# A decoder step on one core: dense activations kept in PSUM, low halves moved to GpSimd, and a gather tile with one buffer fewer

## The chip, the cores and the metric

One Trainium2 chip, one of its cores. The metric is the device time of one execution in microseconds (us), the median of several runs. In the text PE is the matrix engine, DVE the vector engine, ACT the scalar engine, POOL the GpSimd engine and SP the queue that issues most loads.

## What is computed

A decoder layer for 1024 prompt tokens and 8 samples of 8 tokens (1088 tokens, 9 tiles: 0 to 7 are prompt, 8 is the 64 sample tokens): RMSNorm, two recurrent mixers (retention and RWKV-7) with one output projection, then the PEER expert mixer, then a gated per-layer input, then a final norm. The change lies in the PEER part:

```
def block(xb):
    q = (xb @ wq).reshape(PEER_BLOCK, PEER_HEADS, 2, PEER_DKEY // 2)
    s = jnp.einsum('phcd,hcnd->phcn', q, keys)
    sv, si = lax.top_k(s, PEER_TOPK)
    ...                        # the best 16 of 16 x 16 pairs give e, an expert number out of 16384
    gsm = jax.nn.softmax(cv, axis=-1)
    hval = jnp.einsum('pd,phkd->phk', xb, u_tab[e])
    act = gelu(hval) * gsm
    return jnp.einsum('phk,phkd->pd', act, v_tab[e])
```

Each token picks 8 x 16 experts; each expert is a row of 1024 numbers in `u_tab` (peer_u) and one in `v_tab` (peer_v).

## The kernel before

All data are fp32; a product that must be exact to fp32 is made of three fast products of a high and a low half (`mm3`, L325 to L327). A half pair comes from `split` (L296 ACT copies to the rounded type, then L298 on DVE or L300 on POOL subtracts to get the low half).

The PEER part is done in two ways:

- **Gathered.** For tiles 0, 1, 8 (list `E0`, run by `early` beside the mixers) and 2, 3 (`G1`, run later), `gather` fetches for each of a token's 128 experts one row per token by an indirect DMA that POOL issues (L1127, 128 rows of 4 KB into a buffer `grow`), and DVE multiplies and sums it (L1141 for peer_u, L1155 for peer_v; the running sum `gacc` lies in PSUM). Tile 8 needs 64 rows a table, the others 128. In all 576 rows of each table. The buffers that `grow` rotates through are shared with the query and top-k work of the early tiles: tile 0 uses the tags V (two buffers), W and xy, tiles 1 and 8 those and xT, which is also the buffer of the transposed input in the query of tile 8 and of `eq` in its top-k.
- **Dense.** For tiles 4 to 7 (`G2`, 512 tokens) all 128 x 128 experts are multiplied and weighted by a mostly zero gate matrix. `hidden` makes gelu(u x) for 128 experts at once (24 matmuls into `ph`, L1265 gelu to `geh`). The first 96 of the 128 blocks (`NPRE`) are made early and stored to DRAM (`gd`). `gates` builds the gate matrix of a tile in 32 steps of 4 tokens: two one-hot tiles on DVE (L1241), four scalings on ACT (L1243), four matmuls `pwt` (L1246), one copy (L1247), and stores it to DRAM (`wd`). Its SBUF pool `gw` opens where the early gather's pool is closed, and its first copy (`it`, L1234) follows. Then `dense_fused` makes the last 32 blocks and uses them at once; `dense_stored` loads the 96 others again (`ge`). `act` multiplies by the gate (L1275) and splits into `ah` and `al` (L296, L298); `dense` loads a piece of peer_v (`vraw`), splits it into `vh` and `vl`, and multiplies (`py`, L1300: 12 matmuls each in the fused part, 15 in the stored one, 224 `py` in all), and DVE adds `py` to `yT` (L1307).

`ple` is the last part. The program is written as generators; a scheduler of the language puts the instructions of each engine in an order by priority (the order of the text) and by its own costs, and that order is then fixed. On the chip each engine runs its list in order and waits on semaphores. An SBUF buffer of a closed pool is handed on tile by tile, with a wait.

Of the kernel before, what the change touches and what calls it, by code (L numbers as in the profile page):

```python
# [8 lines left out]
F32 = mybir.dt.float32  # L9
# [162 lines left out]
GHB = 2  # L172
# [38 lines left out]
class K:  # L211
# [117 lines left out]
    def group(self, tiles):  # L329
        self.tiles = tiles  # L330
        self.off, self.ntok = spans(tiles)
        self.chunks = chunks_of(self.ntok)
# [878 lines left out]
    def early(self, wp):  # L1211

        rows = ("V", "V", "W", "xy")
        yield from self.early_query(wp, E0[0], "V", 2, ("W", "Wq"))
        g = self.gather(wp, E0[0], rows, acc=self.acc)
        for t in E0[1:]:
            while t not in self.rowed:
                next(g, None)
                yield
            for _ in self.early_query(wp, t, "Wq", 1, ("Wq", "xT")):  # L1220
                next(g, None)
                yield
        yield from g
        for t in E0[1:]:
            yield from self.gather(wp, t, rows + ("xT",), acc=self.acc)
# [26 lines left out]
    def hidden(self, dp, ep, x, i1):  # L1252

        nc, I = self.nc, self.I
        ch = self.chunks
        raw = dp.tile([128, 8, 128], F32, name="uraw", bufs=UB)
        nc.sync.dma_start(raw, I['puT'][i1])
        uh = dp.tile([128, 8, 128], F32R, name="uh", bufs=DW)
        ul = dp.tile([128, 8, 128], F32R, name="ul", bufs=DW)
        self.split(uh, ul, raw, "g")  # L1260
        ge = ep.tile([128, self.ntok], F32, name="geh", bufs=GHB)
        for c0, cn in ch:
            p = self.psh.tile([128, 512], F32, name="ph")
            self.mm3(p[:, :cn], lambda k: uh[:, k, :], lambda k: ul[:, k, :], lambda k: x[0][:, k, c0:c0 + cn], lambda k: x[1][:, k, c0:c0 + cn], 8)
            nc.scalar.activation(ge[:, c0:c0 + cn], p[:, :cn], AF.Gelu)  # L1265
        return ge

    def act(self, dl, dr, i1, ge):
        nc = self.nc
# [11 lines left out]
    def dense(self, dl, dr, yT, groups, acts_of, side):  # L1281
        nc, I = self.nc, self.I
        ch = self.chunks
        cw = ch[0][1]
        ncx = len(ch)
        for g0, nb in groups:
            acts = acts_of(g0, nb)
            for d in range(8):
# [5 lines left out]
                self.split(vh, vl, raw, "g" if d % 2 else "v")  # L1294
                p = self.ps2.tile([128, ncx, 512], F32, name="py")
                for b in range(nb):
                    ah, al = acts[b]
                    for j, (lh, rh) in enumerate(((vh, ah), (vh, al), (vl, ah))):
                        for c, (c0, cn) in enumerate(ch):
                            nc.tensor.matmul(p[:, c, :cn], lh[:, b, :], rh[:, c0:c0 + cn], start=b == 0 and j == 0,  # L1300
                                             stop=b == nb - 1 and j == 2)
                pv = p[:, :ncx, :cw]
                yv = yT[:, d, :].rearrange("p (c n) -> p c n", c=ncx)
                if self.first:
                    nc.vector.tensor_copy(yv, pv)
                else:
                    nc.vector.tensor_tensor(yv, yv, pv, op=OP.add)  # L1307
            self.first = False

    def dense_fused(self, dl, dr, hp, x, yT):  # L1310
# [112 lines left out]
    def build(self):  # L1423
# [3 lines left out]
        with self.es:  # L1427
# [94 lines left out]
            with ExitStack() as e:  # L1522
                dl = sb("dl", e, bufs=2)
                yT = sb("dy", e, side="right").tile([128, 8, self.ntok], F32, name="yT")
                with ExitStack() as e2:
                    self.ps2 = self.pool("psumy", bufs=4 // len(self.chunks), space=PS, es=e2, reuse_waits="tile")
                    dr = sb("dr", e2, bufs=2, side="right")
                    with ExitStack() as e3:
                        self.psh = self.pool("psumh2", bufs=2, space=PS, es=e3, reuse_waits="tile")
                        self.dense_fused(dl, dr, da, x, yT)  # L1530
# [20 lines left out]
```

## Time and profile before

| | |
|---|---|
| median of 3 runs | 4120.41 us (4110.44 to 4128.16) |
| the profiled execution | 4119.08 us, of which the span from first to last instruction is 4117.0 us |
| mean granted PE clock | 0.858 |
| busy over the span | PE 84%, DVE 77%, POOL 54%, ACT 28% |
| DMA | 1107 MB, 269 GB/s over the span |

An engine's busy time counts its own instructions, not its waits. PE's matmuls overlap one another, so that a group's mean duration (0.4 us) is longer than the distance from one to the next (0.23 us); a sum over PE is therefore made from counts per microsecond. The parts of the span, by the first matmul of each kind: the mixers, the early tiles and the query of the others to 1997 us; hidden products, top-k and gates to 2953 us; the fused dense part to 3265 us; the stored part to 3949 us; the last part to 4117 us.

### The profile page before, as it was taken

What the parts mean: (1) busy time and instruction counts of PE and PEld (TensorE: products, weight loads), DVE (VectorE), ACT (ScalarE), POOL (GpSimd) and SP (SyncE); (2) the same over time, 40 slices, a digit from 0 to 9 for tenths busy, and PEclk for the clock granted to TensorE, in tenths of its full rate; (3) what the DMA queues carried; (4) which work ended last, traced back from release to release, by engine and by line L of the source; (5) the groups of instructions that cost most, each with busy time, mean ns of one, the idle gap of its engine ahead of it and who ended that gap; (6) DMA issues with size and microseconds to landing.
All of it is one profiled execution on the core that took longest, in us unless ns stands there. A gap on an engine that the chain in (4) does not pass through costs nothing. (4 is left out here: it accounts for less than half of the span.)

```text
span 4117.0 us, 52401 instructions
## 1 busy us (share of the span) xinstructions
PE 3449.2 (84%) x17749; PEld 2831.4 (69%) x17749; DVE 3165.3 (77%) x5876; ACT 1172.9 (28%) x2149; POOL 2212.5 (54%) x1939
## 2 busy tenths in 40 slices
PE   8789977777779888849998989856699988888988
PEld 7688976546658766638877767745588766666767
DVE  4453579877881588776799988898799989999844
ACT  4232211111111111112222325767422222222222
POOL 5353265544451155545678888643477666666410
PEclk9799986577775678769999999866799999999999
DMA  7267478899772368899988888888899999999822
GB/s 254 77 205 231 143 254 271 280 285 289 262 245 81 102 215 303 301 347 342 335 266 311 300 292 301 322 323 301 302 325 339 333 339 352 351 350 361 311 90 68
DMA packets 473862, 1107.18 MB, mean 269 GB/s; under 512 B 74555, under 2 KB 191545, under 8 KB 467642
## 3 DMA queue, kind: packets, MB, share of 16 engines
q0 software_dynamic: 165888, 604.05, 41.3%
q1 hardware_dynamic: 245694, 393.26, 29.3%
q10 hardware_dynamic: 62012, 106.52, 7.0%
q8 instruction: 140, 2.29, 0.2%
q14 instruction: 128, 1.05, 0.1%
HBM read 997.17 MB, written 106.43 MB: 268 GB/s over the span
## 5 line engine op out<-in xcount | busy, mean ns | idle before, releaser
L1127 POOL DMA_INDIRECT grow<-in_pv,eid x576 | 588.2, 1021 | 529.8 <-DVE gacc L1155 359.7
L1127 POOL DMA_INDIRECT grow<-in_pu,eid x576 | 580.2, 1007 | 480.7 <-DVE grow L1141 342.3
L1155 DVE SCALAR_TENSOR_TENSOR gacc<-grow,ac,gacc 128x1024 f32<-128x1024 f32 x571 | 732.4, 1283 | 109.7 <-DMA grow<-in_pv,eid 103.5
L1141 DVE SCALAR_TENSOR_TENSOR grow<-grow,gacc 128x1024 f32<-128x1024 f32 x576 | 689.5, 1212 | 57.8 <-DMA grow<-in_pu,eid 53.4
L1300 PE MATMUL py<-ah,vl 128*128 128x512 f32 x1024 | 412.1, 408 | 49.4 <-DVE vl L298 32.0
L1300 PE MATMUL py<-ah,vh 128*128 128x512 f32 x1024 | 413.0, 407 | 38.4 <-ACT ah L296 25.2
L325 PE MATMUL ph<-cx,uh 128*128 128x512 f32 x1024 | 409.8, 400 | 23.2 <-ACT geh L1265 14.7
L327 PE MATMUL ph<-cx,ul 128*128 128x512 f32 x1024 | 406.6, 399 | 19.5 <-POOL ul L300 19.5
L1300 PE MATMUL py<-al,vh 128*128 128x512 f32 x1024 | 411.5, 402 | 3.1 <-DVE al L298 3.1
L326 PE MATMUL ph<-cx,uh 128*128 128x512 f32 x1024 | 406.4, 397 | 0.0
L300 POOL TENSOR_TENSOR ul<-uraw,uh 128x1024 fp32r<-128x1024 f32 x128 | 307.2, 2401 | 29.5 <-ACT uh L296 27.5
L1246 PE MATMUL pwt<-oh,oh 128*128 128x128 f32 x1024 | 202.5, 365 | 122.8 <-ACT oh L1243 105.1
L1246 PEld LDWEIGHTS pwt<-oh,oh 128*128 128x128 f32 x1024 | 182.9, 260 | 143.9 <-ACT oh L1243 141.8
L1300 PEld LDWEIGHTS py<-ah,vl 128*128 128x128 f32 x1024 | 196.6, 192 | 118.8 <-DVE vl L298 51.8
L1300 PEld LDWEIGHTS py<-ah,vh 128*128 128x128 f32 x1024 | 197.4, 193 | 100.7 <-ACT vh L296 32.7
L325 PEld LDWEIGHTS ph<-cx,uh 128*128 128x128 f32 x1024 | 196.7, 192 | 68.7 <-ACT geh L1265 17.4
L327 PEld LDWEIGHTS ph<-cx,ul 128*128 128x128 f32 x1024 | 196.6, 192 | 67.7 <-POOL ul L300 26.4
L300 POOL TENSOR_TENSOR vl<-vraw,vh 128x640 fp32r<-128x640 f32 (+2 forms) x112 | 171.1, 1527 | 128.8 <-ACT vh L296 126.1
L296 ACT ACTIVATE uh<-uraw 128x1024 fp32r<-128x1024 f32 x128 | 135.5, 1059 | 360.3 <-DMA uraw<-in_puT 276.9
L1300 PEld LDWEIGHTS py<-al,vh 128*128 128x128 f32 x1024 | 197.1, 193 | 50.7 <-DVE al L298 8.0
L296 ACT ACTIVATE vh<-vraw 128x640 fp32r<-128x640 f32 (+2 forms) x224 | 149.6, 686 | 272.8 <-PE py L1300 202.5
L326 PEld LDWEIGHTS ph<-cx,uh 128*128 128x128 f32 x1024 | 197.1, 192 | 41.2
(402 smaller groups left out, 7959.7 us busy)
## 6 DMA issues: line engine op xcount, KB each, us to landing
uraw<-in_puT SPq DMA_DIRECT2D x128, 512.0 KB, 5.0
vraw<-in_pvd SPq DMA_DIRECT2D x152, 320.0 KB, 5.3
cw<-in_w_out SPq DMA_DIRECT2D x128, 256.0 KB, 5.3
wd<-wst ACTq DMA_DIRECT2D x32, 1024.0 KB, 11.2
wt<-wd SPq DMA_DIRECT2D x64, 512.0 KB, 6.7
wraw<-in_w_ret SPq DMA_DIRECT2D x48, 512.0 KB, 4.8
ewq<-in_wq SPq DMA_DIRECT2D x48, 512.0 KB, 4.4
gd<-geh ACTq DMA_DIRECT2D x96, 256.0 KB, 5.1
```

The source lines that it names most:

```text
L296: nc.scalar.activation(hi, src, AF.Copy)
L300: nc.gpsimd.tensor_tensor(lo, src, hi.bitcast(F32), op=OP.subtract)
L325: mm(out, lh(k), rh(k), start=first and k == 0, stop=False)
L326: mm(out, lh(k), rl(k), start=False, stop=False)
L327: mm(out, ll(k), rh(k), start=False, stop=last and k == nk - 1)
L1127: nc.gpsimd.indirect_dma_start(out=g, out_offset=None, in_=src, in_offset=bass.IndirectOffsetOnAxis(ap=self.eid[t][:, j:j + 1], axis=0))
L1141: nc.vector.scalar_tensor_tensor(g[:, c], g[:, c], 1.0, x[:, c], op0=OP.mult, op1=OP.mult, accum_out=hv[:, i, j:j + 1])
L1155: nc.vector.scalar_tensor_tensor(y[:, c], g[:, c], ac[:, j:j + 1], y[:, c], op0=OP.mult, op1=OP.add)
L1246: nc.tensor.matmul(pw[:, j, :], oh[1][:, j, :], oh[0][:, j, :], start=True, stop=True)
L1300: nc.tensor.matmul(p[:, c, :cn], lh[:, b, :], rh[:, c0:c0 + cn], start=b == 0 and j == 0, stop=b == nb - 1 and j == 2)
```

## The change

Three things are done at once.

1. **Tile 1's gather** no longer takes a fifth buffer with the tag xT; tile 8's still does. Tile 1 now rotates through four.
2. **Activations from PSUM.** In the fused part the gelu writes back into its PSUM tile `ph`, and the gate product and the split read it there. In the stored part the loaded `ge` is first copied by ACT into such a PSUM tile (a new instruction for each of 96 blocks). There are three `ph` and three `py` PSUM tiles in the whole dense part; before there were two `ph` in the fused part alone and four `py`. In the hidden stage (96 blocks) the gelu still goes to SBUF.
3. **peer_v's low halves** `vl` are all made by POOL. Before, DVE and POOL took every other one (112 each).

```diff
@@ early
         for t in E0[1:]:
-            yield from self.gather(wp, t, rows + ("xT",), acc=self.acc)
+            yield from self.gather(wp, t, rows + ("xT",) * (t == E0[-1]), acc=self.acc)
@@ hidden
-        ge = ep.tile([128, self.ntok], F32, name="geh", bufs=GHB)
-        for c0, cn in ch:
-            p = self.psh.tile([128, 512], F32, name="ph")
...
-            nc.scalar.activation(ge[:, c0:c0 + cn], p[:, :cn], AF.Gelu)
+        p = self.psh.tile([128, self.ntok], F32, name="ph")
+        self.mm3(p, lambda k: uh[:, k, :], lambda k: ul[:, k, :], lambda k: x[0][:, k], lambda k: x[1][:, k], 8)
+        ge = ep.tile([128, self.ntok], F32, name="geh", bufs=GHB) if ep else p
+        nc.scalar.activation(ge, p, AF.Gelu)
@@ dense
-                self.split(vh, vl, raw, "g" if d % 2 else "v")
+                self.split(vh, vl, raw, "g")
@@ dense_fused
-                made[b] = self.act(dl, dr, b, self.hidden(hp, dr, x, b))
+                made[b] = self.act(dl, dr, b, self.hidden(hp, None, x, b))
@@ dense_stored
                 self.nc.sync.dma_start(ge, self.gd[b])
-                out.append(self.act(dl, dr, b, ge))
+                p = self.psh.tile([128, self.ntok], F32, name="ph")
+                self.nc.scalar.activation(p, ge, AF.Copy)
+                out.append(self.act(dl, dr, b, p))
@@ build
-                    self.ps2 = self.pool("psumy", bufs=4 // len(self.chunks), space=PS, es=e2, reuse_waits="tile")
+                    self.ps2 = self.pool("psumy", bufs=3, space=PS, es=e2, reuse_waits="tile")
+                    self.psh = self.pool("psumh2", bufs=3, space=PS, es=e2, reuse_waits="tile")
```

What this does to the order of the instructions is shown at three places.

**POOL, in the mixers, behind the last rows of tile 0** (`eid_65` is the list of tile 1's experts; hnr, kk, k, rk, Z, hnx and the like belong to the mixers). Before, four rows of tile 1 are issued, then none until the query and top-k of tile 8 are through:

```order
L1127 DMA grow<-in_pu,eid_65 128x1024 x4
L290 TENSOR_SCALAR crs<-cssq 128x1
L736 COPY pe<-Pa 128x4
L735 COPY pe<-Pi 128x4
L291 TENSOR_TENSOR crs<-crs,halves 128x1
L745 TENSOR_TENSOR kk<-ft,vec 128x512
L752 TENSOR_TENSOR k_9766<-ft,m_9761 128x512
L756 TENSOR_TENSOR rk_9770<-ft,vec 128x512
L757 TENSOR_TENSOR rk_9770<-rk_9770,k_9766 128x512
L783 TENSOR_TENSOR k_9766<-k_9766,Pi 128x512
```

With the change, a little further down the same stretch:

```order
L1126 DMA grow<-in_pu,eid_65 128x1024 x18
L290 TENSOR_SCALAR hnr<-hnss 128x8
L291 TENSOR_TENSOR hnr<-hnr,halves 128x8
L1126 DMA grow<-in_pu,eid_65 128x1024 x3
L970 TENSOR_TENSOR hnx<-hnx,row_ln_g 128x512
L1126 DMA grow<-in_pu,eid_65 128x1024
L971 TENSOR_TENSOR hnx<-hnx,row_ln_b 128x512
L1126 DMA grow<-in_pu,eid_65 128x1024
L974 TENSOR_TENSOR hnx<-hnx,bv 128x512
L825 TENSOR_TENSOR Z<-Z,csta 128x1024
L1126 DMA grow<-in_pu,eid_65 128x1024 x67
```

Rows of tile 1 fill the stretch in which there were none. Where the first hidden block's low half stands on POOL, 577 rows have been issued, 472 before. Where the first `vl` stands, it is 777 rows, 799 before.

**PE, in the hidden stage, at the second tile's gates** (`ph` are hidden products, `pit` the transposed gate input of a tile, `pwt` the gate products). Before, 2018 of the `ph` matmuls stand ahead of the first `pwt`, and here all of the 96 hidden blocks are already done, so that the `pwt` follow each other:

```order
L326 MATMUL ph<-cx_13026,uh 128x512
L327 MATMUL ph<-cx_13025,ul 128x512
L1246 MATMUL pwt<-oh_17197,oh_17198 128x128
L1232 MATMUL pit<-csta,e_17212 128x128 x2
L1232 MATMUL pit<-csta,gsm 128x128
L1246 MATMUL pwt<-oh_17197,oh_17198 128x128 x3
L1246 MATMUL pwt<-oh_18860,oh_18861 128x128 x4
```

With the change 847 `ph` stand ahead of the first `pwt`, and the gates lie between hidden products:

```order
L325 MATMUL ph<-cx_13025,uh 128x512
L326 MATMUL ph<-cx_13026,uh 128x512
L1245 MATMUL pwt<-oh_17197,oh_17198 128x128 x4
L1231 MATMUL pit<-csta,e_17212 128x128 x2
L1231 MATMUL pit<-csta,gsm 128x128
L327 MATMUL ph<-cx_13025,ul 128x512
L325 MATMUL ph<-cx_13025,uh 128x512
L326 MATMUL ph<-cx_13026,uh 128x512
```

From the first `pwt` to the last there are now some 1529 `ph`; the last 60 of the 512 `pwt` stand alone. On DVE the first gate instruction stands, in both programs, just behind the last row of tile 8.

**POOL, in the stored dense part** (`vl` low halves, `grow` rows of tile 3, `eid_68`, `pgb` weights of the last part). Before, one `vl` for two to three rows:

```order
L300 TENSOR_TENSOR vl<-vraw,vh 128x640
L1127 DMA grow<-in_pv,eid_68 128x1024 x2
L300 TENSOR_TENSOR pgb<-pgr,pgb 128x512
L1127 DMA grow<-in_pv,eid_68 128x1024 x3
L300 TENSOR_TENSOR vl<-vraw,vh 128x640
```

With the change:

```order
L300 TENSOR_TENSOR vl<-vraw,vh 128x640
L1126 DMA grow<-in_pv,eid_68 128x1024
L300 TENSOR_TENSOR vl<-vraw,vh 128x640 x2
L1126 DMA grow<-in_pv,eid_68 128x1024 x2
L300 TENSOR_TENSOR vl<-vraw,vh 128x640
```

Two `vl` for each one, and the rows reach to the end: sixteen rows of tile 3 stand behind the last `vl`; before, the last row stood at the 98th of POOL's 112 `vl`.

More of the change, by code (lines that the diff above doesn't have):

```diff
@@ L331, in group @@
         self.off, self.ntok = spans(tiles)
-        self.chunks = chunks_of(self.ntok)
     def a_pool(self, es, name):
@@ L1254, in hidden @@
         nc, I = self.nc, self.I
-        ch = self.chunks
         raw = dp.tile([128, 8, 128], F32, name="uraw", bufs=UB)
@@ L1260, in hidden @@
         self.split(uh, ul, raw, "g")
-        ge = ep.tile([128, self.ntok], F32, name="geh", bufs=GHB)
-        for c0, cn in ch:
-            p = self.psh.tile([128, 512], F32, name="ph")
-            self.mm3(p[:, :cn], lambda k: uh[:, k, :], lambda k: ul[:, k, :], lambda k: x[0][:, k, c0:c0 + cn], lambda k: x[1][:, k, c0:c0 + cn], 8)
-            nc.scalar.activation(ge[:, c0:c0 + cn], p[:, :cn], AF.Gelu)
+        p = self.psh.tile([128, self.ntok], F32, name="ph")
+        self.mm3(p, lambda k: uh[:, k, :], lambda k: ul[:, k, :], lambda k: x[0][:, k], lambda k: x[1][:, k], 8)
+        ge = ep.tile([128, self.ntok], F32, name="geh", bufs=GHB) if ep else p
+        nc.scalar.activation(ge, p, AF.Gelu)
         return ge
@@ L1282, in dense @@
         nc, I = self.nc, self.I
-        ch = self.chunks
-        cw = ch[0][1]
-        ncx = len(ch)
         for g0, nb in groups:
@@ L1293, in dense @@
                 vl = dl.tile([128, NB, 128], F32R, name="vl")[:, :nb]
-                self.split(vh, vl, raw, "g" if d % 2 else "v")
-                p = self.ps2.tile([128, ncx, 512], F32, name="py")
+                self.split(vh, vl, raw, "g")
+                p = self.ps2.tile([128, self.ntok], F32, name="py")
                 for b in range(nb):
@@ L1298, in dense @@
                     for j, (lh, rh) in enumerate(((vh, ah), (vh, al), (vl, ah))):
[L1299 to L1303, printed above, removed]
+                        nc.tensor.matmul(p, lh[:, b, :], rh, start=b == 0 and j == 0, stop=b == nb - 1 and j == 2)
                 if self.first:
-                    nc.vector.tensor_copy(yv, pv)
+                    nc.vector.tensor_copy(yT[:, d, :], p)
                 else:
-                    nc.vector.tensor_tensor(yv, yv, pv, op=OP.add)
+                    nc.vector.tensor_tensor(yT[:, d, :], yT[:, d, :], p, op=OP.add)
             self.first = False
@@ L1525, in build @@
                 with ExitStack() as e2:
-                    self.ps2 = self.pool("psumy", bufs=4 // len(self.chunks), space=PS, es=e2, reuse_waits="tile")
+                    self.ps2 = self.pool("psumy", bufs=3, space=PS, es=e2, reuse_waits="tile")
+                    self.psh = self.pool("psumh2", bufs=3, space=PS, es=e2, reuse_waits="tile")
                     dr = sb("dr", e2, bufs=2, side="right")
-                    with ExitStack() as e3:
-                        self.psh = self.pool("psumh2", bufs=2, space=PS, es=e3, reuse_waits="tile")
-                        self.dense_fused(dl, dr, da, x, yT)
+                    self.dense_fused(dl, dr, da, x, yT)
                     self.dense_stored(dl, dr, yT, self.ple_weights(cx, da, dl))
```

## The prediction

> **What bounds the kernel now.** I read the span by stages first (engine busy time, granted clock, DMA share), then how many gather rows POOL issues in each, then the waits and the groups of the two stages that the change touches.
>
> ```profile
> core 0: us, PE busy (x) PEld busy (x) DVE busy (x) ACT busy (x) POOL busy (x), PEclk, DMA share, GB/s
> 1219.00:1480.00 261.00, 227.02 (x1073) 191.63 (x1073) 117.05 (x351) 37.22 (x92) 56.15 (x51) 0.61 0.31 100
> 1997.00:2523.00 526.00, 480.04 (x2028) 387.06 (x2027) 488.23 (x1546) 151.88 (x193) 430.54 (x309) 0.97 0.87 297
> 2523.00:2953.00 430.00, 291.52 (x1419) 255.29 (x1417) 373.24 (x581) 299.22 (x675) 222.09 (x201) 0.75 0.86 311
> 2953.00:3265.00 312.00, 307.85 (x1320) 249.33 (x1321) 299.02 (x297) 90.08 (x140) 224.84 (x177) 0.99 0.92 328
> 3265.00:3868.00 603.00, 526.99 (x2086) 394.99 (x2085) 558.62 (x706) 160.94 (x248) 382.92 (x315) 0.96 0.99 353
> 3868.00:3949.00 81.00, 80.31 (x347) 63.83 (x345) 48.54 (x70) 24.73 (x40) 18.43 (x15) 1.00 0.51 159
> 3949.00:4117.00 168.00, 141.13 (x641) 110.78 (x640) 81.97 (x120) 43.74 (x81) 13.40 (x36) 0.93 0.24 79
> ```
>
> Each row is a stage: its length, each engine's busy time (instructions), granted clock, DMA share and rate. The fused part (2953 to 3265) is PE's, 308 of 312 us. The stored part is DVE's up to 3868 (93%), with the DMA engines at 0.99; the 81 us behind it, where the gather is over, run at PE's pace, 347 matmuls in 81 us, 4.28 a us. The hidden stage is two things: up to 2523 PE and DVE are both over 90%, and after it PE is busy for 68% at a clock of 0.75. The stretch from 1219 to 1480 leaves DVE at 45% and DMA at 0.31; POOL's gather line, with its rows in brackets, says why:
>
> ```profile
> core 0: us, POOL busy (x), PEclk, DMA share, GB/s
> 536.00:1219.00 683.00, 261.33 (x256) 0.71 0.84 273
> 1219.00:1480.00 261.00, 3.90 (x4) 0.61 0.31 100
> 1480.00:1997.00 517.00, 216.92 (x225) 0.83 0.90 324
> 1997.00:2523.00 526.00, 161.97 (x156) 0.97 0.87 297
> 2523.00:2953.00 430.00, 156.85 (x163) 0.75 0.86 311
> 2953.00:3265.00 312.00, 128.50 (x125) 0.99 0.92 328
> 3265.00:3949.00 684.00, 238.97 (x224) 0.97 0.93 330
> ```
>
> Four rows in 261 us: tile 1's gather waits for the buffer of tile 8's query. The price is paid later. The gates begin when tile 8's last row is summed (timeline of DVE, then the one-hot and gate instructions of the whole trace, then the waits from 2630 to 2924):
>
> ```profile
> 2513.95 1.29 DVE L1155 SCALAR_TENSOR_TENSOR gacc<-grow,ac,gacc 128x1024 f32<-128x1024 f32 x1 [2.96 <-DMA grow<-in_pv,eid]
> 2517.60 0.28 DVE L1234 COPY it<-pit 128x128 f32<-128x128 f32 x1
> ```
>
> ```profile
> L1246 PE MATMUL pwt<-oh,oh x1024: 270/377/584, 2523.4 to 2923.3; 128*128 128x128 f32 x171
> ```
>
> ```profile
> PEld pwt L1246 <- ACT oh L1243: 132.5, 76, 5.9
> PE pwt L1246 <- ACT oh L1243: 97.3, 65, 5.3
> ```
>
> The hidden products are used up by then, and PE waits 230 us for ACT's scalings with nothing to put between. This is the largest hole in the program.
>
> **The change, part by part.** I sum against the profiled execution: span 4117.0 us, 4119.08 with what lies around it, 1.3 us under the median of 4120.41.
>
> *Gather brought forward.* The order has 577 rows issued at the first hidden block, 472 before; 261 us at the 2.30 us a row of 1480 to 1997 would be 113. What it costs the mixers: DVE and DMA have room, but loads and mixer steps now meet row traffic. The nearest rows are a query beside the gather (906 to 1066, tile 1) and one without (1237 to 1387, tile 8):
>
> ```profile
> 1237.00:1387.00 150.00, 66.23 (x288) 58.55 (x288) 7.89 (x32) 0.55 0.24 75
> 906.00:1066.00 160.00, 50.52 (x252) 44.65 (x252) 7.70 (x28) 0.76 0.87 277
> ```
>
> 288 records in 150 us against 252 in 160, so 183 for 288: up to 33 us more, and 0 where the chain of mixer steps is what sets the pace. Tile 1 also rotates through four buffers; tile 0, with four, took 2.67 us a row, and 320 rows at that take 854 us from 1219, 61 past the 1997 plus 15 that I would else have. I take +20 us up to the first hidden product (0 to 60).
>
> *The hidden stage.* 847 hidden products now stand ahead of the first gate. 2018 of them took 526 us (3.84 a us), so 847 take 221. Then 1529 hidden products and all gates. PE alone: 1529 / 4.28 = 357 us, and the gates by their rows between 2523 and 2625, where hidden products filled the gaps:
>
> ```profile
> 2523.00:2625.00 102.00, 30.77 (x216) 29.69 (x216) 27.71 (x26) 0.98 0.92 325
> ```
>
> 30.77 / 216 = 0.1425 us a record, 146 us for 1024. In that window 286 hidden products (the last of the 96 blocks, by the order) and these 216 records make 97.6 us of PE work in 102, 96%; so (357 + 146) / 0.96 = 524. The last 15 of 128 gate steps stand alone; at the old pace of 300 us for 104 steps they take 43, of which 17 are counted: +26. The stage is 221 + 524 + 26 = 771 us instead of 956: -185. Is DVE able to? It was busy for 861 of 956 us; 119 rows leave (319 to 200), at 1.29 us: 708 of 771 us, 92% where it had 90%. So it fits, barely. Bounds: PE's floor, 221 + 503 (-232), and DVE at 85%, 833 us (-123).
>
> *Activations from PSUM.* The groups of DVE in the dense stage, 2953 to 3949:
>
> ```profile
> L1155 DVE SCALAR_TENSOR_TENSOR gacc<-grow,ac,gacc 128x1024 f32<-128x1024 f32 x224 | 287.3, 1282 | 3.3 <-DMA grow<-in_pv,eid 0.7
> L1307 DVE TENSOR_TENSOR yT<-yT,py 128x512 f32<-128x512 f32 x215 | 145.5, 681 | 54.1 <-PE py L1300 53.8
> L1275 DVE TENSOR_TENSOR ge<-ge,wt 128x512 f32<-128x512 f32 x96 | 87.4, 916 | 8.8 <-DMA ge<-gd 8.8
> L298 DVE TENSOR_TENSOR al<-ge,ah 128x512 fp32r<-128x512 f32 x96 | 82.7, 865 | 12.7 <-ACT ah L296 11.9
> L298 DVE TENSOR_TENSOR vl<-vraw,vh 128x640 fp32r<-128x640 f32 x76 | 74.6, 981 | 0.0
> L1275 DVE TENSOR_TENSOR geh<-geh,wt 128x512 f32<-128x512 f32 x31 | 52.1, 1682 | 3.1 <-ACT geh L1265 3.1
> L298 DVE TENSOR_TENSOR al<-geh,ah 128x512 fp32r<-128x512 f32 x32 | 45.7, 1429 | 1.7 <-ACT ah L296 0.9
> ```
>
> The same size with one operand in PSUM (`yT`) takes 681 ns; with both in SBUF 865 to 1682. The spread says that it is a wait and not the work:
>
> ```profile
> L1307 DVE TENSOR_TENSOR yT<-yT,py x216: 669/680/690, 3012.5 to 3949.5; 128x512 f32<-128x512 f32 x108
> L1275 DVE TENSOR_TENSOR geh<-geh,wt x32: 678/686/3559, 2951.4 to 3270.0; 128x512 f32<-128x512 f32 x32
> ```
>
> The minimum of `geh` is that of `yT`, its maximum 3559 ns. The Trainium skill (SBUF — State Buffer, Who interferes with whom) has the rule: DVE with two SBUF inputs shuts out, and is shut out by, a POOL operation that reads SBUF, and with at most one it is not. The trace agrees, with `yT` never over 690 ns. From `yT` the gate products and low halves take 0.68 us each from PSUM: -23 and -18 us of DVE in the stored part, -31 and -24 in the fused one. ACT's 96 added copies take under 1029 ns each, the 1024-wide ACT write into PSUM:
>
> ```profile
> L1135 ACT ACTIVATE gacc<-gx x5: 1004/1029/1037, 382.2 to 3204.1; 128x1024 f32<-128x1024 f32 x5
> ```
>
> At about half of it that is 55 us on an ACT that is busy for 186 of 684; I cost it at nothing, and without that cover it would be the 55. `py` has three buffers instead of four: DVE still has two `py`, 30 matmuls or 7 us, and in this stage it is DVE that waits for `py` (53.8 us above); nothing, and 0.7 us a `py` (one `yT` addition) if not. The two `ge` buffers come free after ACT's copy, sooner than after `al`, so SP's loads of them can only start earlier.
>
> *Low halves of peer_v to POOL.* POOL's groups in the same stage:
>
> ```profile
> L1127 POOL DMA_INDIRECT grow<-in_pv,eid x221 | 232.8, 1053 | 150.8 <-DVE gacc L1155 106.8 <-PE py L1300 16.6 <-issue 12.1
> L300 POOL TENSOR_TENSOR vl<-vraw,vh 128x640 fp32r<-128x640 f32 x76 | 126.8, 1669 | 95.8 <-ACT vh L296 94.6
> L300 POOL TENSOR_TENSOR ul<-uraw,uh 128x1024 fp32r<-128x1024 f32 x26 | 62.5, 2405 | 4.6 <-ACT uh L296 4.0
> L300 POOL TENSOR_TENSOR vl<-vraw,vh 128x512 fp32r<-128x512 f32 x31 | 41.1, 1325 | 10.6 <-ACT vh L296 10.3
> ```
>
> The stored part: DVE 607 us less 80 x 0.98, less 41, is 488. POOL 401 plus 80 x 1.67 is 535. PE's floor is 2433 / 4.28 = 568 us. DMA is what is late next: 603 x 0.99 + 81 x 0.51 = 638 us of it, for about as many rows (they now reach to the end, so the PE-only tail goes). PE's waits for `vl` (stored part) are these already:
>
> ```profile
> PEld py L1300 <- DVE vl L298: 46.4, 36, 3.3
> PEld py L1300 <- POOL vl L300: 25.0, 21, 4.3
> ```
>
> The first goes, the second may double, since a `vl` now stands behind rows in every `py` and the rows behind it. I take 650 us instead of 684, -34, nearer to the DMA row than to PE's floor; ends 600 and 690. By the HBM share of about 358 GB/s a core that the Trainium skill gives (DMA: Bandwidth & Descriptors, Specifications) the 684 x 330 GB/s would take 630 us, an estimate, and by its 425 for a core alone (Measured) 531, so PE would bind; the trace's 353 at a share of 0.99 lies on the first. The fused part stays at 312: PE has no hole in it, and POOL goes from 225 to 268 us of 312.
>
> *The last part.* Sixteen rows of tile 3 lie behind the last `vl`: at 1.3 us on a DVE that is half idle, +3 us (0 to 20); `ple` takes tile 3 last.
>
> Sum: +20 - 185 - 34 + 0 + 3 = -196, so 4119 - 196 = 3923 us in the profiled execution's terms and 3924 as a median.
>
> **Rivals.**
>
> *The gates stay starved in part.* PE runs one fixed list; where a gate's ACT or DVE step is late, the hidden products behind it wait too. For it: DVE is needed for 92%. Against: from 2523 to 2625 the same mixture ran at 96%. Half the gain lost: +92, 4016 us.
>
> *The dense stage falls to PE's floor*, if a DMA share of 0.99 is not a wall: DVE waited for `ge` only 8.8 us. 568 instead of 650: 3842 us.
>
> *The hole does not close.* If rows arrive at 2.67 us or slower, tile 8 ends as late and the gates start where they did. 4119 + 20 - 34 = 4105 us: no measurable change. Against: at 2.67 it ends 61 us late, not 300.
>
> *POOL becomes the dense bound, and the kernel slower.* POOL does things in order. If its own waits stay with each instruction (95.8 / 76 = 1.26 us a `vl`, 0.68 a row), a stored `vl` costs 2.93 and a row 1.73: 160 x 2.93 + 224 x 1.73 = 856 us instead of 650, and 64 x 1.67 + 125 x 1.73 + 62 for the hidden low halves = 385 instead of 312. Together +279: 4203 us. It decides once the dense stage is 180 us longer than its 996. For it: PE's 25 us for POOL above. Against: a `vl` waited for `vh`, which waits for PE, so POOL is ahead and those waits shrink when it is not.
>
> **How the numbers follow.** Forecast as summed 0.62, partly starved 0.13, PE's floor 0.13, no closing 0.06, POOL the bound 0.06. The likeliest gives 3924, its own range 3870 to 3985. The range that leaves out no more than the last two and some edges is 3835 to 4020. Half a per cent (20 us) is about what a measurement of this kernel can tell from no change: faster 0.88, same 0.07, slower 0.05.
>
> **What would show it.** POOL's rows in 1219 to 1480 go from 4 to about 100. The first `pwt` comes some 220 us behind the first hidden product, and the first `py` some 770. `pwt`'s wait for ACT falls from 230 us to under 80. Gate products and `al` in the dense stage have one duration, near 0.68 us. DVE in the stored part is under 80% busy and DMA's share stays over 0.95. I am wrong if first `py` less first hidden product is over 850 us, or if PE's waits for POOL's `vl` in the dense stage exceed 150 us.

## The result and the profile after

| | before | after |
|---|---|---|
| median | 4115.42 us (4100.54 to 4128.16, 4 runs) | 3941.15 us (3932.92 to 3946.40, 4 runs) |
| the profiled execution | 4119.08 us, span 4117.0 | 3941.76 us, span 3940.0 |
| mean granted PE clock | 0.858 | 0.870 |
| first hidden product | 1997.6 us | 2054.2 us |
| hidden stage (to the first `py`) | 955 | 765 |
| fused part | 312 | 311 |
| stored part | 684 | 639 |
| last part | 168 | 171 |

The ratio is 0.9576, with a 95% interval of 0.9538 to 0.9614; 3924 us had been forecast. By stages, engine busy time, clock and DMA share of the changed kernel are:

```profile
core 0: us, PE busy (x) PEld busy (x) DVE busy (x) ACT busy (x) POOL busy (x), PEclk, DMA share, GB/s
1219.00:1480.00 261.00, 210.31 (x984) 177.15 (x983) 188.93 (x482) 34.83 (x87) 124.19 (x134) 0.59 0.83 287
2054.00:2270.00 216.00, 198.08 (x854) 161.38 (x852) 207.50 (x819) 62.31 (x78) 156.27 (x111) 0.97 0.80 274
2270.00:2819.00 549.00, 490.87 (x2562) 415.85 (x2562) 480.26 (x1113) 385.49 (x786) 373.37 (x273) 0.96 0.81 296
2819.00:3130.00 311.00, 310.79 (x1343) 254.09 (x1344) 238.22 (x261) 93.19 (x142) 254.38 (x211) 0.99 0.95 338
3130.00:3690.00 560.00, 516.97 (x2118) 395.73 (x2117) 430.07 (x630) 207.77 (x339) 431.21 (x357) 0.98 1.00 358
3690.00:3769.00 79.00, 74.70 (x316) 58.98 (x315) 62.81 (x72) 24.43 (x42) 60.16 (x56) 0.99 0.90 317
3769.00:3940.00 171.00, 140.44 (x640) 109.22 (x639) 104.78 (x140) 44.71 (x82) 31.89 (x52) 0.92 0.39 129
```

The stretch from 1219 to 1480, which had a DMA share of 0.31, has 0.83. The second half of the hidden stage, which ran at a PE clock of 0.75 with PE busy for 68%, is at 0.96 and 89%. The stored part has lost its tail without a gather, and its DMA share is 1.00 for 560 us. POOL's gather line alone, with the rows in brackets:

```profile
1219.00:1480.00 261.00, 97.94 (x102) 0.59 0.83 287
1480.00:2054.00 574.00, 231.58 (x232) 0.79 0.86 305
2054.00:2819.00 765.00, 190.85 (x191) 0.96 0.81 290
3130.00:3769.00 639.00, 213.25 (x225) 0.99 0.99 352
```

102 rows in the stretch that had four, and 191 instead of 319 in the hidden stage. PE's waits there (2054 to 2819: us in total, times, longest; PEld is PE's weight load, which overlaps its matmuls) answer to the 230 us of before:

```profile
PE pwt L1245 <- ACT oh L1242: 31.6, 35, 2.9
PEld pwt L1245 <- ACT oh L1242: 46.8, 46, 3.3
```

The prediction added two such rows of before, 97.3 for PE and 132.5 for PEld, to 230 us. They overlap and can't be added as time, as the stretch that they come from shows: of its 294 us PE was busy for 179, so it stood idle for 115.

```profile
2630.00:2924.00 294.00, 178.81 (x848) 159.29 (x846) 272.25 (x438) 215.47 (x503) 127.81 (x126) 0.67 0.83 303
```

By the same sum the rows after make 78; PE's own row falls from 97.3 to 31.6 us.

In the dense stage (2819 to 3769) the groups of DVE, ACT and POOL that the change touches are now (busy us in all and mean ns of one, then the engine's idle time just before them and what ended it):

```profile
L1298 DVE TENSOR_TENSOR yT<-yT,py 128x512 f32<-128x512 f32 x214 | 146.2, 684 | 151.5 <-PE py L1294 151.1
L1273 DVE TENSOR_TENSOR ph<-ph,wt 128x512 f32<-128x512 f32 x127 | 87.6, 694 | 50.0 <-ACT ph L1262 47.6 <-ACT ph L1328 2.3
L298 DVE TENSOR_TENSOR al<-ph,ah 128x512 fp32r<-128x512 f32 x128 | 86.6, 685 | 8.8 <-ACT ah L296 8.3
L1328 ACT ACTIVATE ph<-ge 128x512 f32<-128x512 f32 x96 | 56.3, 589 | 4.6 <-DVE al L298 3.8 <-DMA ge<-gd 0.6
L300 POOL TENSOR_TENSOR vl<-vraw,vh 128x640 fp32r<-128x640 f32 x152 | 238.5, 1575 | 34.2 <-ACT vh L296 32.2
L1126 POOL DMA_INDIRECT grow<-in_pv,eid x229 | 217.5, 950 | 85.2 <-DVE gacc L1154 31.9 <-issue 24.8 <-PE py L1294 16.1
```

Gate products and low halves, 865 to 1682 ns before, are at 685 to 694 like `yT`; of all 128 gate products none is drawn out any more (ns: least, median, most):

```profile
L1273 DVE TENSOR_TENSOR ph<-ph,wt x128: 683/693/700, 2817.8 to 3734.2; 128x512 f32<-128x512 f32 x128
```

DVE waits 151 us for `py` in the dense stage (54 before) and is busy for 77% of the stored part (89% before): it is not the bound any more.

### The profile page after: what moved, and what is told of

It reads as the page before. It is cut to its first block, busy times and chain, and to the rows that moved or that the text cites. A ratio compares the mean times of both kernels' runs of the same rounds, so it can differ in the third digit from the quotient of the medians.

```text
span 3940.0 us, 52682 instructions
## 1 busy us (share of the span) xinstructions
PE 3367.7 (85%) x17749; PEld 2768.7 (70%) x17749; DVE 2961.7 (75%) x5764; ACT 1225.5 (31%) x2247; POOL 2339.6 (59%) x2051
## 4 chain that ended last, share of the span: by engine, by line
PE 45%; DVE 22%; DMA 16%; issue 7%; POOL 6%; ACT 2%; SPq 0%; ACTq 0%; POOLq 0%; DVEq 0%
PE py L1294 14%; DVE grow L1140 4%; DVE gacc L1154 3%; PE ph L325 3%; PE ph L326 3%; PE ph L327 3%; POOL grow L1126 3%; DMA ewq<-in_wq 2%; PE epq L1194 2%; DMA grow<-in_pv,eid 2%; DMA grow<-in_pu,eid 2%; POOL vl L300 2%; DMA ft<-fd 1%; DVE oh L1240 1%; PE ewo L610 1%
## 5 line engine op out<-in xcount | busy, mean ns | idle before, releaser
L1126 POOL DMA_INDIRECT grow<-in_pv,eid x576 | 569.8, 989 | 507.3 <-DVE gacc L1154 309.4
L1126 POOL DMA_INDIRECT grow<-in_pu,eid x576 | 568.7, 987 | 435.2 <-DVE grow L1140 287.9
L300 POOL TENSOR_TENSOR vl<-vraw,vh 128x640 fp32r<-128x640 f32 (+2 forms) x224 | 325.4, 1457 | 53.1 <-ACT vh L296 49.3
L1294 PEld LDWEIGHTS py<-ah,vl 128*128 128x128 f32 x1024 | 194.1, 190 | 98.4 <-POOL vl L300 56.1
L1298 DVE TENSOR_TENSOR yT<-yT,py 128x512 f32<-128x512 f32 x216 | 147.4, 684 | 151.5 <-PE py L1294 151.1
L300 POOL TENSOR_TENSOR wl<-wraw,wh 128x1024 fp32r<-128x1024 f32 x45 | 110.5, 2455 | 138.8 <-ACT wh L296 138.7
```

What stands on the lines that cost most here:

```text
L300: nc.gpsimd.tensor_tensor(lo, src, hi.bitcast(F32), op=OP.subtract)
L1126: nc.gpsimd.indirect_dma_start(out=g, out_offset=None, in_=src, in_offset=bass.IndirectOffsetOnAxis(ap=self.eid[t][:, j:j + 1], axis=0))
L1294: nc.tensor.matmul(p, lh[:, b, :], rh, start=b == 0 and j == 0, stop=b == nb - 1 and j == 2)
L1298: nc.vector.tensor_tensor(yT[:, d, :], yT[:, d, :], p, op=OP.add)
```

## The experiments

All medians are compared with runs of the kernel before on the same chip. "Rows" counts DVE's row sums that start between the first hidden product and the first `py`; times are us, those of the stages from the one profiled execution. e7, e8 and e11 leave work out and don't give the layer's result; they are there to measure with.

| kernel | median | ratio to before (95%) | first hidden product | hidden stage | rows in it | stored |
|---|---|---|---|---|---|---|
| before | | 1 | 1997.6 | 955 | 315 | 684 |
| after | 3941.2 | 0.958 (0.954 to 0.961) | 2054.2 | 765 | 188 | 639 |
| e1, part 1 alone | 3991.0 | 0.971 (0.968 to 0.974) | 2045.6 | 768 | 189 | 704 |
| e2, part 2 alone | 4088.3 | 0.995 (0.993 to 0.997) | 1979.5 | 960 | 316 | 662 |
| e3, part 3 alone | 4149.6 | 1.007 (1.004 to 1.010) | 1997.7 | 950 | 316 | 722 |
| e4, parts 2 and 3 | 4063.0 | 0.986 (0.982 to 0.991) | 1997.6 | 960 | 316 | 639 |
| e5, tile 8 later | 4022.3 | 0.977 (0.971 to 0.983) | 1995.2 | 792 | 207 | 703 |
| e6, tile 2 earlier | 3964.0 | 0.963 (0.958 to 0.968) | 2059.1 | 793 | 212 | 640 |
| e7, query weights once | 3937.2 | 0.956 (0.952 to 0.961) | 2025.3 | 793 | 200 | 638 |
| e8, half the v loads | 3882.8 | 0.943 (0.939 to 0.947) | 2056.7 | 766 | 188 | 577 |
| e9, three buffers | 4007.2 | 0.979 (0.973 to 0.984) | 2073.0 | 828 | 228 | 639 |
| e10, 88 stored | 3944.4 | 0.964 (0.959 to 0.970) | 2041.7 | 753 | 186 | 585 |
| e11, fewer one-hots | 3945.8 | 0.962 (0.960 to 0.964) | 2029.9 | 771 | 190 | 641 |
| e12, casts moved | 3922.0 | 0.955 (0.953 to 0.958) | 2050.6 | 751 | 188 | 637 |

### The three parts apart

e1 is the kernel before with `rows + ("xT",) * (t == E0[-1])` alone:

> The kernel before with part 1 of the change alone: tile 1's gather leaves the xT buffer alone. My theory, that this part alone closes the hole in the hidden stage: first hidden product about 2054 us (57 later than before), first py about 765 us behind it (956 before), the gate products begin about 215 us behind the first hidden product (526 before); the dense part stays DVE's and holds some 22 rows more, so it is 0 to 28 us longer than before. In all 3980 to 4010 us, a gain of 105 to 135 of the 174. Rival, that the hole closes only with a lighter DVE in the dense part: 4090 to 4115 us. Rival, that DVE in the dense part gives everything back: 4050 us or more.

e2 has the activations in PSUM, with tile 1's fifth buffer and the alternating split left as before:

> The kernel before with part 2 alone: dense activations gated and split from PSUM, three ph and three py buffers, peer_v's low halves still made by DVE and POOL in turn. My theory: gate products and al take 0.68 to 0.69 us each, DVE loses 41 us in the stored part, which goes from 684 to 650 to 665 us; the fused part stays at 312; nothing changes ahead of 2953 us. In all 4085 to 4100 us. Rival, that DVE's mere share was no limit and DMA is: no change, 4110 to 4120. Rival, that three py buffers hold PE back: slower, over 4120, with PE waiting for yT.

e3 changes the split alone:

```diff
-                self.split(vh, vl, raw, "g" if d % 2 else "v")
+                self.split(vh, vl, raw, "g")
```

> The kernel before with part 3 alone: all of peer_v's low halves on POOL, activations still in SBUF. My theory: DVE loses 104 us of its own work in the dense part, but POOL's subtractions double and hold up DVE's operations with two SBUF inputs (ge, al, geh) for longer, so these grow from 0.9 to 1.7 us a piece to over 1.2 and 2; the dense part gains 0 to 30 us: 4085 to 4115. Rival, no contention worth naming: the full relief, 4070 or less. Rival, POOL becomes the bound: 4130 or more.

e4 is the changed kernel with tile 1's five buffers:

> The change without part 1 (tile 1 keeps its fifth buffer xT): parts 2 and 3 together. My theory, that the parts add up: first hidden product and hidden stage as before (1997 and 956 us), stored part 640 to 650 instead of 684: 4070 to 4085 us. Rival, that the dense parts also shorten the hidden stage: under 4050.

The hidden stage is part 1's alone: 768 us in e1, 950 to 960 in e2 to e4. e1 gains 124 us and e4 52 against 4114.66 us of the kernel before, 176 together; the whole change gained 174. e1 and e2 came as expected (in e2's profiled execution, though, 18 us lie in the mixers, which part 2 doesn't touch, and 22 in the stored part); e4's 4063 us lie 7 under its range. Parts 2 and 3 hang together. e3 is a miss: part 3 alone is slower, not up to 30 us faster, and its stored part takes 722 us instead of 684. DVE's groups of e3, from first to last `py`, with the gate products and low halves still in SBUF:

```profile
L298 DVE TENSOR_TENSOR al<-ge,ah 128x512 fp32r<-128x512 f32 x96 | 124.7, 1301 | 28.8 <-ACT ah L296 24.3 <-issue 2.8
L1275 DVE TENSOR_TENSOR ge<-ge,wt 128x512 f32<-128x512 f32 x96 | 103.0, 1076 | 6.6 <-DMA ge<-gd 4.1 <-DMA wt<-wd 2.4
L298 DVE TENSOR_TENSOR al<-geh,ah 128x512 fp32r<-128x512 f32 x32 | 69.5, 2175 | 2.8 <-ACT ah L296 1.4
L1275 DVE TENSOR_TENSOR geh<-geh,wt 128x512 f32<-128x512 f32 x30 | 39.3, 1311 | 3.2 <-ACT geh L1265 3.1
```

With twice the POOL subtractions beside them, `al` from `ge` goes from 865 to 1301 ns, `ge` from 916 to 1076, `al` from `geh` from 1429 to 2175; only the gate product of `geh` falls, from 1682 to 1311. The four groups took 267.9 us before and take 336.5 here, so 69 of the 104 us that DVE was to lose came back. With one operand in PSUM (e4 and after, 684 to 694 ns) nothing of this is left. The rule of the Trainium skill (SBUF — State Buffer, Who interferes with whom), that a DVE instruction with two SBUF inputs contends with a POOL instruction that reads SBUF, agrees with these durations.

What makes e3's stored part longer is shown less well. PE's matmuls wait there for POOL's `vl`:

```profile
PE py L1300 <- POOL vl L300: 68.5, 51, 4.6
```

Before it was 16.1 us for POOL's and 29.7 for DVE's `vl`, and in e4, with the same subtractions on POOL, 40.0 us. POOL was busy for 72% of e3's stored part and DVE for 83%, so neither fills it with work alone. e4 differs from e3 by part 2, and part 2 also changes the number of `py` buffers and when `ge` comes free: that the drawn-out operations cost the time is likely, and not separated from these.

### Where the gates begin, and what the hidden stage costs

e5 is the kernel before, with tile 8's peer_v and peer_u rows gathered after the queries instead of beside the mixers:

```diff
-            yield from self.gather(wp, t, rows + ("xT",), acc=self.acc)
+            if t != 8:
+                yield from self.gather(wp, t, rows + ("xT",), acc=self.acc)
...
                             run(self.topk(tp, t))
+                            if t == G1[0]:
+                                run(self.behind(self.gather(gp, 8, acc=acc), PG))
```

> The kernel before, with tile 8's gather taken out of the early part and run ahead of tile 2's instead; tile 1 keeps its fifth buffer, nothing is brought forward, no row is left out. It tells whether the end of the early gather sets the start of the gates, or the number of rows. My theory, the end: with tile 1's last row the gates may start, 195 us behind the first hidden product (747 hidden products stand ahead of the first gate product), the hidden stage takes 760 to 790 us instead of 955, and the mixers stay at 1997; the 108 rows that so move behind the hidden stage cost the dense part and the last part some of it back: 3980 to 4050 us in all. Rival, that the hole closed because rows came forward into idle time: gates start over 400 us behind the first hidden product, hidden stage over 900 us, 4100 or more.

The mixers are those of before (1995 us), yet the gates start 193 us after the first hidden product, where before they took 526, and the hidden stage falls to 792 (760 to 790 were expected). So it was the end of the early gather that held the gates back, and not anything that a shorter or longer mixer part does. The 24 to 27 us that it lies above e1 and the changed kernel go with 18 or 19 more rows in the stage; the postponed rows come back in the stored part (703) and the last one (227).

e6 starts tile 2's top-k and gather one tile earlier in the hidden stage:

```diff
-TK1 = {2: 1, 3: 4}
+TK1 = {2: 0, 3: 4}
```

> The changed kernel with the top-k and the gather of tile 2 put one step earlier, into the stretch from 2238 to 2381 us in which no row is issued; 24 more rows stand ahead of the dense part. My theory: the dense part is the transfers' and loses 24 x 1.4 = 34 us, the hidden stage gains up to 30 us since DVE is busy for 90% of it: 3915 to 3945 us. Rival, that the hidden stage has DVE to spare: 3905 or less. Rival, that more rows beside top-k and gates open the hole again: 3960 or more.

A miss: 24 rows more in the hidden stage cost 28 us there, and the stored part didn't move (640). The median of 3964 us lies where the second rival had it, though the gates start as early as in the changed kernel (220 us behind the first hidden product).

e9 gives tile 1 three buffers (V, V and W), so that its rows come later:

```diff
-rows + ("xT",) * (t == E0[-1])
+rows + ("xT",) if t == E0[-1] else rows[:3]
```

> The changed kernel, with tile 1's gather rotating through three buffers (V, V, W) instead of four. In its order 547 rows are issued at the first hidden block (577), and 1251 hidden products stand ahead of the first gate (847). My theory, that the end of the early gather sets where the gates begin, and that the hidden stage is PE's as long as enough hidden products are left to stand between gates: the gates start 280 to 330 us after the first hidden product instead of 216, and the stage still takes 750 to 790 us. If rows in flight beside the mixers are what costs them the 27 us that the query's weights do not explain, the first hidden product moves from 2054 to 2030 to 2045 us, and the median is 3915 to 3940. Rival: the mixers' cost is in the order of the work and not in the rows in flight (2050 to 2060 us), and each row that is late comes back in the hidden stage, DVE being the one that is late there: 3950 to 3990 us.

Both expectations missed. The gates start 329 us behind the first hidden product, as computed, but the stage grows to 828 us with 40 more rows, and the mixers get longer instead of shorter (2073 us).

From after (188 rows, 765 us) to before (315 rows, 955 us) a row in the hidden stage costs 190 / 127 = 1.50 us. On that line e5 would take 793 us (measured 792), e6 801 (793), e7 783 (793), e9 825 (828). The line holds to 10 us, whether the gates start 193 or 329 us behind the first hidden product.

Where the time goes shows when the stage is cut at the last hidden product that stands ahead of the last gates: behind the cut PE has little but gate products left. The two stretches of before, of after, of e9 and of e10 (which comes below) are:

```profile
1998.00:2641.00 643.00, 589.22 (x2608) 481.14 (x2607) 584.15 (x1692) 238.73 (x374) 521.28 (x379) 0.97 0.87 301
2641.00:2953.00 312.00, 181.34 (x831) 160.26 (x829) 276.35 (x433) 211.67 (x492) 131.02 (x131) 0.67 0.84 308
```

```profile
2054.00:2762.00 708.00, 666.86 (x3296) 557.92 (x3294) 649.32 (x1877) 414.62 (x784) 509.04 (x363) 0.98 0.81 289
2762.00:2819.00 57.00, 22.09 (x120) 19.30 (x120) 38.45 (x54) 33.18 (x81) 20.61 (x20) 0.72 0.78 302
```

```profile
2073.00:2755.00 682.00, 631.39 (x3028) 526.88 (x3027) 636.22 (x1822) 346.98 (x623) 520.11 (x375) 0.97 0.84 292
2755.00:2901.00 146.00, 75.47 (x390) 67.36 (x389) 114.24 (x170) 101.15 (x244) 47.53 (x49) 0.73 0.81 298
```

```profile
2041.00:2686.00 645.00, 606.50 (x2973) 505.42 (x2972) 605.45 (x1801) 367.26 (x683) 470.92 (x335) 0.98 0.80 281
2686.00:2795.00 109.00, 52.26 (x256) 46.12 (x256) 81.59 (x130) 68.49 (x165) 37.40 (x38) 0.67 0.85 312
```

Ahead of the cut PE is busy for 92 to 94% in all four (92 to 96% in all of the kernels), behind it for 39 to 58%. The second stretch is what makes a stage long: 312 us before, 57 after, 146 in e9, and 88 to 91 in e5, e6 and e7. Rows that are late on DVE make the gates late, and then more of them are left when the hidden products are used up. So part 1 closes the hole that the prediction named, and the 1.50 us a row is how that shows in the count of rows. What paces the lone gates isn't separated: DVE, with rows and one-hots, is busy for 89% of that stretch before and for 67% after.

In all of e1 to e10 DVE was busy for 0.89 to 0.92 of the stage, so DVE's work is a rival cause. e11 takes 64 of 256 one-hot instructions from DVE alone:

```diff
-                oh = [wp.tile([128, 4, 128], F32, name=f"oh{j}", bufs=2) for j in range(2)]
-                for j in range(2):
+                oh = [wp.tile([128, 4, 128], F32, name="oh0", bufs=2),
+                      wp.tile([128, 4, 128], F32, name="oh1", bufs=2) if b % 8 == 0 else oh[1]]
+                for j in range(2 if b % 8 == 0 else 1):
```

> The changed kernel, in which a gate step uses the second one-hot tile of the step before in every second step, so 64 of DVE's 256 one-hot instructions in the hidden stage are left out (the gate matrices are then not those of the reference; PE, ACT, POOL and the transfers have the same work). 64 x 0.677 = 43 us less for DVE. My theory now: in the ten kernels run so far DVE was busy for 0.89 to 0.92 of the hidden stage, whatever its length (753 to 960 us), so DVE's work sets it: 688 - 43 = 645, by 0.905 713 us; PE's matmuls alone need 701 to 724 us there, so 715 to 735 instead of 765, and a median of 3890 to 3912. Rival, that of my prediction: the stage goes at PE's pace with ACT's scalings between (PE busy for 0.90 as well): then a DVE with less to do changes it by under 10 us: 755 to 765, median 3930 to 3945.

The hidden stage of e11:

```profile
2030.00:2801.00 771.00, 690.13 (x3415) 581.50 (x3414) 650.60 (x1869) 447.15 (x864) 529.63 (x385) 0.95 0.81 288
```

DVE is busy for 651 instead of 688 us, 0.84 of a stage that is no shorter. So DVE's work alone doesn't set the stage: up to the cut PE is busy for 666 of 710 us, 94% as in the changed kernel, and the lone gates take 61 us. The time went into DVE's waits: 53.5 us for `pwt` before a one-hot (31.3 in after) and 24.4 for row landings (11.1). e12 leaves nothing out and moves other work off DVE, for the six tiles whose top-k lies in the stage:

```diff
-        nc.vector.tensor_copy(sf[:n]...
+        (nc.vector.tensor_copy if tags else nc.scalar.copy)(sf[:n]...
...
-        for src, dst, eng in ((svv, cand, nc.vector), (sf, eid, nc.gpsimd)):
+        for src, dst, eng in ((svv, cand, nc.vector if tags else nc.gpsimd), (sf, eid, nc.gpsimd)):
...
-        nc.vector.tensor_copy(cf[:n], ci...
+        (nc.vector.tensor_copy if tags else nc.scalar.copy)(cf[:n], ci...
...
-            nc.vector.tensor_copy(self.e12[t][:n], e1[:n])
+            nc.scalar.copy(self.e12[t][:n], e1[:n])
```

> The changed kernel with nothing left out; in the top-k of the six tiles whose top-k lies in the hidden stage, three conversions (sf, cf and e12) go from DVE to ACT and the sums of candidates from DVE to POOL. By the rows of the changed kernel that is 4.9 + 10.4 + 9.1 + 23.5 = 48 us less for DVE, some 6 us more for ACT (busy for 448 of 765) and some 13 more for POOL (530 of 765), and the top-k now waits for two queues more. If DVE's work sets the hidden stage: 688 - 48 = 640, by 0.905 707 us, under PE's 701 to 724, so 715 to 735 instead of 765 and a median of 3890 to 3912. If DVE is not what sets it, or waits for ACT and POOL as long as it saves, the stage stays at 755 to 775 and the median at 3930 to 3950.

The stage is 751 us, between the two expectations. DVE is busy for 669 us, 19 less and not 48; part of the rest went into the `eq` instructions (two SBUF inputs), which took 1222 ns before this edit:

```profile
L1081 DVE TENSOR_TENSOR eq<-csta,cf 128x800 f32<-128x800 f32 x48 | 69.7, 1452 | 0.2
```

Its six runs (3910.16 to 3926.00) lie under the four of the changed kernel, but weren't taken beside them (the kernel before had 4104.80 us there and 4115.42 here), and the ratios to before, 0.955 and 0.958, have intervals that overlap: perhaps the better version, not shown to be. Its 14 us lie ahead of the cut, where PE is busy for 664 of 693 us, 96%, instead of 667 of 708.

### The mixers' loss

e7 takes away one thing that part 1 slowed: in the query of tile 8 the weights are loaded once instead of 16 times.

```diff
-            w = wp.tile([128, 8, 128], F32, name="ewq", tag=wtag, bufs=wbufs)
-            nc.sync.dma_start(w, I['wq'][hc])
+            if t != 8 or hc == 0:
+                w = wp.tile([128, 8, 128], F32, name="ewq", tag=wtag, bufs=wbufs)
+                nc.sync.dma_start(w, I['wq'][hc])
```

> The changed kernel with the weights of tile 8's query loaded once and used for all 16 half heads: 15 loads of 512 KB are left out (tile 8 so picks other experts; as many rows). It tells where the 57 us in the mixers come from. My theory, the query's single weight buffer, whose load lands in 6.9 us beside the rows and in 3.5 without them: the query falls from 177 us to under 150, and the first hidden product comes at 2015 to 2030 instead of 2054. Rival, DVE waiting for rows in its fixed list: 2045 or later.

The query of tile 8 took 149 us before, 178 after, and 136 here. (It takes 145 to 149 in the kernels whose mixers are those of before, 172 to 179 in those that have the changed kernel's.) Its weight has one buffer, so that each load's landing lies in its path; the loads of that stretch, first before and then after (us from issue to landing):

```profile
ewq<-in_wq SPq DMA_DIRECT2D x15, 512.0 KB, 3.5
```

```profile
ewq<-in_wq SPq DMA_DIRECT2D x15, 512.0 KB, 6.9
```

15 x 3.4 = 51 us more of landing, of which 29 show in the query. The first hidden product comes 29 us earlier than in the changed kernel (2025 us; kernels with the changed kernel's mixers spread over 2030 to 2059, so the query's own time is the firmer figure), and the kernel is no faster: the early gather, with nothing of its own sped up, ends no earlier (2278 us; 2261 after), 12 more of its rows fall into the hidden stage, and that grows by 28 us. The rest of the mixers' loss goes with DVE's waits for rows from 1219 to 1871 us, of before, after and e9:

```profile
DVE grow L1141 <- DMA grow<-in_pu,eid: 15.5, 18, 2.5
DVE gacc L1155 <- DMA grow<-in_pv,eid: 11.7, 11, 3.0
```

```profile
DVE grow L1140 <- DMA grow<-in_pu,eid: 44.0, 35, 3.3
DVE gacc L1154 <- DMA grow<-in_pv,eid: 18.9, 19, 3.7
```

```profile
DVE grow L1140 <- DMA grow<-in_pu,eid: 84.4, 59, 3.6
DVE gacc L1154 <- DMA grow<-in_pv,eid: 44.6, 38, 3.9
```

27, 63 and 129 us with five, four and three buffers for tile 1, while the first hidden product goes from 1998 to 2054 and 2073. DVE takes its list in order, so a mixer step behind a row waits with it. In e7, whose query is short, these waits are 64 us (63 in the changed kernel), and the first hidden product is still 28 us behind that of before. The two don't move one for one (66 us more of waits in e9 go with 19 us), so this cause is likely and not shown. A separate fifth buffer for tile 1, or a second one for the query's weight, wasn't tried.

### The wall of the stored part

e8 loads every other piece of peer_v only and uses it twice:

```diff
-                raw = dl.tile([128, NB, 128], F32, name="vraw", bufs=VB)[:, :nb]
-                nc.sync.dma_start(raw, I['pvd'][d, :, g0:g0 + nb])
+                if d % 2 == 0:
+                    raw = dl.tile([128, NB, 128], F32, name="vraw", bufs=VB)[:, :nb]
+                    nc.sync.dma_start(raw, I['pvd'][d, :, g0:g0 + nb])
```

> The changed kernel with every second load of a piece of peer_v left out (two products share one, so the dense sum is of other weights); every other instruction is there. In the stored part 26 of 225 MB go. My theory, that the transfers are the wall there (share 1.00): the stored part falls from 639 to 570 to 600 us, DMA's share falls under 0.95, and PE's floor of 568 is near. Rival, that POOL's and DVE's waits are the wall and a share of 1.00 is not: 630 or more.

Its stored part, and PE's wait for POOL's `vl` there:

```profile
3133.00:3710.00 577.00, 566.74 (x2430) 455.73 (x2429) 476.39 (x677) 232.50 (x382) 479.78 (x399) 0.99 0.96 332
```

```profile
PE py L1295 <- POOL vl L300: 3.1, 5, 1.3
```

With the same POOL and DVE work and fewer loads, 639 us become 577, PE is busy for 98%, and PE's matmul waits for `vl`, 34.0 us in after, are 3.1. So those waits came of the peer_v loads and not of POOL's speed. What it is about the loads isn't separated. e8 moves fewer bytes, and the DMA share falls from 0.99 to 0.96 (under 0.95 was expected). But each loaded piece also serves two products, and SP's next load waits until POOL's `vl` is done with a buffer; in after:

```profile
SPq L1286 <- POOL vl L300: 290.4, 135, 5.9
```

In e8 it is 215.2 us in 71 waits. Bytes alone don't order the runs: e6 moves 345 GB/s over 640 us, 221 MB, and e7 357 over 638, 228 MB. More peer_v buffers at the same bytes weren't tried, so the transfers as the limit of this part are likely and not shown. e10 moves work of it elsewhere:

```diff
-NPRE = 96
+NPRE = 88
```

> The changed kernel with 88 instead of 96 blocks made early and stored; the other 40 go through the fused part, so nothing is left out. Per block 24 hidden and about 16 py matmuls move into the fused part, and 0.26 MB of stored activations and 0.52 MB of peer_v are no longer loaded in the stored part; by the order about 34 rows (18 MB) move out of it too. My theory, that the transfers are the wall in the stored part and PE in the fused one: stored 639 to 560-585 us (201 of 225 MB at 358 GB/s), fused 311 to 400-410, and in the hidden stage 192 matmuls fewer, 45 us of PE: 765 to 720-735 where PE paces it. Total -5 to -30 us, median 3910 to 3935. Rival: DVE paces the hidden stage (it is busy for 90% of it), so that it stays at 755 to 770, and the sum is +5 to +25 us: 3945 to 3965.

Stored part (585) and fused part (398) came within 2 us of what was computed, the first with a DMA share of 1.01 up to 3700 us:

```profile
3193.00:3700.00 507.00, 468.61 (x1916) 360.15 (x1915) 391.79 (x544) 187.00 (x309) 392.52 (x326) 0.98 1.01 360
```

But 88/96 of 639 us is 586 too, so this run doesn't tell the transfers from any other cost that each block has. The hidden stage lost 12 us instead of 30 to 45, with 192 matmuls fewer and as many rows. That is near the rival's time, but DVE's work, its reason, is what e11 speaks against. The two stretches shown above give another: ahead of the cut the stage is 63 us shorter (645 for 708), but with fewer hidden products to put between more gates are left alone, and these take 52 us more (109 for 57). The three stages together take 1736 us, 21 more than in the changed kernel; the ratio is 0.964 where the change has 0.958, with intervals that overlap: no gain.

## Why the prediction was right

- **Mixers, +20 us forecast, +57 measured.** This is the term that was mis-sized; it lies at the end of its bounds (0 to 60). Its first half, the query beside the gather, was worked out as up to 33 us and measured 29. Its second half, tile 1's rotation through four buffers, was worked out as 61 us late and weighed as if it hit only the gather: by the runs it shows in the mixers too, where DVE's waits for rows went from 27 to 63 us. The two halves add up to 94 us, and the value taken was 20; 57 lies between. Kernels whose mixers are the same as the changed kernel's reached the first hidden product at 2030 to 2059 us and those like before at 1980 to 1998, so the size is known to some 15 us.
- **Hidden stage, -185, measured -190.** Gates 216 us behind the first hidden product (221 forecast), first `py` 765 (771), `pwt`'s wait for ACT 78 us (under 80). DVE was busy for 688 us (708). The 230 us that this wait was to fall from add two overlapping rows; PE's idle time in that stretch was 115 us. The sum doesn't rest on it. The mechanism is borne out: the early gather's end sets the gates' start (e5), gates and hidden products together ran with PE busy for 95% (96%), and then 15 gate steps stood alone. By its parts the forecast was less close than by its sum: 216 us of hidden products (221), 492 of the mixture (507), 30 of lone gates (43), and 27 us more before the first `py`, in which PE waits for ACT's `ah` and which the forecast doesn't have. That these errors add up to 6 us is luck.
- **Fused part, 0, measured -1.** PE was busy for 310.8 of 311 us. POOL needed 254 us there (268 forecast).
- **Stored part, -34, measured -45.** The DMA row alone had given 638 us, and 639 is what it took; the 12 us added towards POOL's waits weren't there. ACT's added copies took 56.3 us (55 estimated), and DVE waited 2.3 us for them, so costing them at nothing was right. PE's waits for POOL's `vl` in this part are:

```profile
PE py L1294 <- POOL vl L300: 34.0, 38, 2.7
PEld py L1294 <- POOL vl L300: 56.1, 53, 3.1
```

  The 25 us that might double were the PEld row alone. It is 56.1, and PE's own row went from 16.1 to 34.0: both a little over the double, and even their sum of 90 is under the 150 named as the limit. The 358 GB/s at a share of 1.00 is the figure of the Trainium skill (DMA: Bandwidth & Descriptors, Specifications) that the prediction set beside the trace.
- **Last part, +3, measured +3.**
- **The sum**: 57 - 190 - 1 - 45 + 3 = -176, and the spans differ by 177. Against the forecast the terms are off by +37, -5, -1, -11 and 0. They partly cancel, which is luck; without it the forecast would have been off by the 37 of the mixers.
- **The rivals.** POOL as the bound: it waited 34.2 / 152 = 0.22 us for a `vl` in the dense stage and not 1.26, so its waits did shrink when it was no longer ahead. PE's floor in the stored part (568) is 9 us under what e8 reached, but with half of the peer_v loads left out: with all of them the part stays at 637 to 641 us in the changed kernel and in e6, e7, e9, e11 and e12. Partly starved gates and no closing did not happen.

## What to carry to other kernels

Before an operation is moved onto POOL, look at what DVE does beside it: the low halves cost 0.7% alone and paid only together with operands in PSUM. When a buffer less lets work start earlier, price what the engine that consumes it in order has behind it, and don't set such a cost near its low end without a reason: here the parts added up to 94 us, 20 was taken and 57 measured. A stage that gets shorter upstream gains nothing if the chain that feeds the next one (here the early gather) ends when it did: in e7 the first hidden product came 29 us earlier and the hidden stage took 28 us longer. And rows of PE and of its weight loads in a table of waits overlap: the engine's busy time shows how much of their sum it really stood idle.

## What was not expected of the hardware

- POOL itself got faster when DVE's instructions with two SBUF inputs went: a `vl` of 128x640 took 1669 ns before and 1575 after, issuing one gather row 1053 and 950. (In e3, where of those instructions only DVE's `vl` went, the `vl` took 1596 and a row 1037 to 1066.) In e12 the reverse showed: with more small sums on POOL, DVE's `eq` went from 1222 to 1452 ns.
- A 512 KB load took 3.5 us from issue to landing at a DMA share of 0.24 and 6.9 beside the gather at 0.83.
